# Column mean on one core: the wait of VectorE's second addition, the leader of the first section, and ScalarE waiting for the last pair's second rows

## The chip, the core and the metric

The kernel runs on one core of a Trainium2 chip. The core's engines each run their own queue of instructions and meet through semaphores: TensorE (PE in the profile; PEld its weight loads), VectorE (DVE), ScalarE (ACT), GpSimd (POOL) and SyncE (SP), which here issues nearly all DMA transfers. An entry such as DVEq is the engine's sequencer: waits, branches, raising of semaphores, drains. The metric is the device time of the program in microseconds (us), as the median of several runs; less is better.

## The reference

```python
def reference(x):            # x: 8192 x 8192, float32
    return np.mean(x, axis=0)
```

## The kernel before

`x` is read once, 268.4 MB. The 8192 rows are 64 slabs of 128 rows. Slabs 0 to 61 are read as 31 pairs: pair k is 256 rows, two to a partition, so that a partition gets 2 x 8192 numbers, the first rows and the second rows, in one tile of 128 x 16384 (`pair0`, `pair1`, `pair2` in turn, three buffers of 8.4 MB). The last two slabs, `slab` and `last`, go into the buffer of pair 28.

SyncE issues the loads (line 85). Pairs 0 to 27 come in one transfer each (pair 0 in two), pairs 28 to 30 in two, first and second rows, the second on semaphores `second[b]`. From pair 3 on each load waits for the semaphore `read` (line 80).

VectorE makes two additions of 128 x 8192 for a pair (helper `add`, line 54). `first_rows(b)` (63) adds the sum so far, which lies in the first half of the buffer before, to the pair's first rows; `second_rows(b)` (67) adds the pair's second rows to that. A running sum thus moves from buffer to buffer. The semaphore `summed` is 1 after a second addition and 0 after a first one, and orders the additions: the first waits for 1 (line 64), the second for 0 (line 68). That wait for 0 is an instruction of its own and also raises `read`: the buffer before may be loaded anew. Pairs 1 to 27 are a loop of 9 turns of three pairs (88 to 92), in which `take` (57) waits for the landing and takes it off the semaphore; pairs 28 and 29 follow unrolled (93 to 97).

The instructions up to there stand in a critical section (line 76), which is opened and closed by one engine for all engines in it: SyncE. At its end the others drain and tell the leader, which lets the work behind the section go on. A second section (line 100), led by VectorE, holds pair 30's first addition and the wait for its second rows.

What follows is in the order of the text, with waits put in by the framework. `behind` (112) puts an instruction behind the second section. SyncE loads `slab` in four pieces (158) and `last` in ten (161, sizes `PIECES`); the later pieces are each issued when an earlier one has landed. VectorE adds pair 30's second rows in four quarters (166), and `slab`'s last quarter to the fourth (168). TensorE sums over partitions by matmuls with a tile of ones (line 130): three wide groups of columns, each 4 x 512, from `before` (pair 30's buffer), `slab` and `last`; a fourth of 4 x 256; four narrow ones of 256 (`fold_wide`, `fold_narrow`, `close`). ScalarE and VectorE scale the sums (145, 147). GpSimd stores the three wide groups (`rw`, 192), SyncE the rest (`r3`, 196; `row`, 208).

Of the kernel before, what the change touches and what calls it, by code (L numbers as in the profile page):

```python
# [22 lines left out]
def kernel(  # L23
# [5 lines left out]
    nc = tc.nc  # L29
    P = nc.NUM_PARTITIONS  # L30
    R, C = x.shape
    n_slabs = R // P
    n_pairs = n_slabs // 2 - 1
# [11 lines left out]
    pairs = [pair_pool.tile([P, 2 * C], F32, name=f"pair{b}", tag=f"pair{b}") for b in range(3)]  # L45


    landed = [tc.alloc_semaphore(f"landed{b}") for b in range(3)]
    second = [tc.alloc_semaphore(f"second{b}") for b in range(BY_ROW)]
    summed = tc.alloc_semaphore("summed")  # L50
    read = tc.alloc_semaphore("read")

    def add(dst, a, b):
        return nc.vector.tensor_tensor(out=dst, in0=a, in1=b, op=ADD)  # L54

    def take(sem, n):
        nc.vector.wait_ge(sem, n).then_inc(sem, -n)  # L57

    def rows(k):
        src = x[2 * P * k : 2 * P * (k + 1), :]  # L60
        return src.rearrange("(p j) c -> p (j c)", j=2)

    def first_rows(b):
        nc.vector.wait_ge(summed, 1)
        add(pairs[b][:, 0:C], pairs[b][:, 0:C], pairs[b - 1][:, 0:C]).then_inc(summed, -1)

    def second_rows(b):
        nc.vector.wait_op(summed, 0, "sem-eq").then_inc(read, 1)
        add(pairs[b][:, 0:C], pairs[b][:, 0:C], pairs[b][:, C : 2 * C]).then_inc(summed, 1)

    n_loop = n_pairs - BY_ROW - 1
    assert n_loop % 3 == 0
    with tc.tile_critical(no_gpsimd_drain=True, sync_engine=mybir.EngineType.SP):
        for k in range(n_pairs):
            b = k % 3
            if k >= 3:
                nc.sync.wait_ge(read, k - 2)  # L80
            cut = FIRST if k == 0 else C if k >= n_pairs - BY_ROW else 2 * C
            for lo, hi in ((0, cut), (cut, 2 * C)):
                if lo < hi:
                    sem = second[b] if lo == C else landed[b]
                    nc.sync.dma_start(out=pairs[b][:, lo:hi], in_=rows(k)[:, lo:hi]).then_inc(sem, 16)
        take(landed[0], 32)
        add(pairs[0][:, 0:C], pairs[0][:, 0:C], pairs[0][:, C : 2 * C]).then_inc(summed, 1)
        with nc.vector.Fori(0, n_loop // 3):
            for b in (1, 2, 0):
                take(landed[b], 16)  # L90
                first_rows(b)
                second_rows(b)
        for k in range(n_loop + 1, n_pairs - 1):
            nc.vector.wait_ge(landed[k % 3], 16)
            first_rows(k % 3)
            nc.vector.wait_ge(second[k % 3], 16)
            second_rows(k % 3)
    last_b = (n_pairs - 1) % 3
    before = pairs[last_b]
    with tc.tile_critical(no_gpsimd_drain=True, sync_engine=mybir.EngineType.DVE) as section:  # L100
        nc.vector.wait_ge(landed[last_b], 16)
        first_rows(last_b)
        nc.vector.wait_ge(second[last_b], 16)
        nc.vector.wait_op(summed, 0, "sem-eq")


    ctx.enter_context(tc.manual_schedule())


    order = mybir.DependencyInfo(mybir.DependencyClass.NoSync, mybir.DependencyReason.DATA)  # L110

    def behind(ins):
        tc.add_manual_dep(ins.ins, section.name, order, reason="not ahead of the section")

    ones = const_pool.tile([P, 32], F32)
    behind(nc.gpsimd.memset(ones, 1.0))  # L116

    wide, lo = [], 0
# [35 lines left out]
    slab, last = tail[:, 0:C], tail[:, C : 2 * C]  # L154
    parts = [(lo, lo + w) for lo, w, _ in wide[:3]] + [(wide[3][0], C)]
    for lo in range(0, C, C // 4):
        hi = lo + C // 4
        behind(nc.sync.dma_start(out=slab[:, lo:hi], in_=x[r : r + P, lo:hi]))
    lo = 0
# [2 lines left out]
        lo += w  # L162


    for lo, hi in parts:
        add(before[:, lo:hi], before[:, lo:hi], before[:, C + lo : C + hi])
    lo, hi = parts[3]
    add(before[:, lo:hi], before[:, lo:hi], slab[:, lo:hi])

# [69 lines left out]
```

## Time and profile before

| what | value |
|---|---|
| median of 3 runs | 629.08 us (628.46 to 629.09) |
| the profiled execution | 629.22 us, span 627.2 us |
| DVE busy | 533.5 us (85%) |
| PE busy | 13.0 us (2%) |
| HBM read | 268.44 MB, mean 428 GB/s |
| additions of 128x8192 | 60, each 8.69 us |
| loads of pairs (line 85), issue to landing | median 29.7 us |
| TensorE's first matmul | 610.88 us |
| SyncE's issue of the last store | 624.47 us |

The span runs from the first to the last instruction that was profiled; times inside it count from its start. Lines give the kernel's source line, the engine, the operation, the tiles, and in brackets the idle time before and what ended it. "Landing" is the last of a transfer's semaphore updates.

### The profile page before, as it was taken

The numbers are of one execution on the slowest core, as the hardware profiler recorded it, in microseconds if no ns is written. First come the engines' busy times: TensorE is split into PE (matmuls) and PEld (weight loads), VectorE is DVE, ScalarE is ACT, GpSimd is POOL, SyncE is SP. The second block draws the span as 40 slices with busy tenths as digits, with TensorE's granted clock in tenths as the row PEclk, the third lists the DMA queues.
The fourth block names the chain that finished last, engine by engine and source line by source line (L and its number), as shares of the span: only waits on it lengthen the run. The fifth ranks groups of instructions, "written<-read, shape, count | busy, mean of one in ns | idle before, by whom it ended". The sixth has DMA issues, their size and how long they took to land. (4 is left out here: it accounts for less than half of the span.)

```text
span 627.2 us, 518 instructions
## 1 busy us (share of the span) xinstructions
PE 13.0 (2%) x108; PEld 4.6 (1%) x108; DVE 533.5 (85%) x67; ACT 4.1 (1%) x7; POOL 1.0 (0%) x6
## 2 busy tenths in 40 slices
PE   0000000000000000000000000000000000000007
PEld 0000000000000000000000000000000000000002
DVE  0538988889888899888898888988889888899995
ACT  0000000000000000000000000000000000000001
POOL 0000000000000000000000000000000000000000
PEclk9999999999999999999999999999999999999999
DMA  9999999999999999999999999999999999999997
GB/s 392 410 468 401 468 401 431 439 401 468 401 468 401 468 401 468 401 468 401 468 401 468 401 468 401 468 401 468 401 468 401 468 401 468 401 435 433 435 409 299
DMA packets 7115, 268.49 MB, mean 428 GB/s; under 512 B 957, under 2 KB 1473, under 8 KB 1866
## 3 DMA queue, kind: packets, MB, share of 16 engines
q1 hardware_dynamic: 7066, 268.45, 99.2%
q0 software_dynamic: 48, 0.02, 0.0%
q8 instruction: 1, 0.02, 0.0%
HBM read 268.44 MB, written 0.03 MB: 428 GB/s over the span
## 5 line engine op out<-in xcount | busy, mean ns | idle before, releaser
L54 DVE TENSOR_TENSOR pair<-pair,pair 128x8192 f32<-128x8192 f32 (+1 forms) x31 | 263.1, 8485 | 59.3 <-DVEq L57 58.3
L54 DVE TENSOR_TENSOR pair<-pair 128x8192 f32<-128x8192 f32 (+1 forms) x34 | 269.6, 7938 | 27.7 <-DVEq L57 22.8
L130 PE MATMUL wide<-pair,ones 128*32 128x512 f32 (+1 forms) x88 | 12.2, 661 | 610.9 <-DVE pair L54 610.9
L130 PEld LDWEIGHTS wide<-pair,ones 128*32 128x32 f32 x88 | 3.6, 126 | 617.9 <-issue 617.2
L145 ACT ACTIVATE rw<-wide 128x512 f32<-128x512 f32 x3 | 1.8, 598 | 619.5 <-PE wide L130 619.5
L147 DVE TENSOR_SCALAR row<-narrow 1x256 f32<-1x256 f32 x2 | 0.8, 416 | 3.9 <-PE narrow L130 3.8
L130 PE MATMUL narrow<-pair,ones 128*32 128x256 f32 (+3 forms) x20 | 3.3, 386 | 0.0
L192 POOL DMA_DIRECT2D out_dram<-rw x1 | 0.7, 697 | 622.7 <-ACT r L145 622.7
L130 PEld LDWEIGHTS narrow<-pair,ones 128*32 128x32 f32 x20 | 1.3, 109 | 1.1 <-issue 0.6
L145 ACT ACT_TABLE_LOAD x1 | 1.3, 1283 | 0.7 <-PEq L223 0.7
L145 ACT ACTIVATE row<-narrow 1x256 f32<-1x256 f32 x2 | 0.8, 376 | 0.0
L145 ACT ACTIVATE r<-wide 128x256 f32<-128x256 f32 x1 | 0.4, 378 | 0.0
L116 POOL MEMSET ones<- 128x32 f32 x1 | 0.1, 125 | 0.3 <-POOLq L223 0.3
L223 POOL MEMSET const-float32-0.0<- 128x1 f32 x1 | 0.1, 98 | 0.2 <-issue 0.2
L223 POOL MEMSET const-float32-1.0<- 128x1 f32 x1 | 0.1, 98 | 0.0
L223 POOL MEMSET const-bfloat16-1.0<- 128x1 bf16 x1 | 0.1, 98 | 0.0
L223 POOL MEMSET const-uint8-127<- 128x1 uint8 x1 | 0.1, 98 | 0.0
## 6 DMA issues: line engine op xcount, KB each, us to landing
pair<-in_x_dram SPq DMA_DIRECT2D x6, 4096.0 KB, 25.5
pair<-in_x_dram SPq DMA_DIRECT2D x7, 1024.0 KB, 11.3
pair<-in_x_dram SPq DMA_DIRECT2D x1, 7168.0 KB, 21.2
pair<-in_x_dram SPq DMA_DIRECT2D x3, 512.0 KB, 16.0
pair<-in_x_dram SPq DMA_DIRECT2D x27, 29.7
pair<-in_x_dram SPq DMA_DIRECT2D x3, 128.0 KB, 11.8
pair<-in_x_dram SPq DMA_DIRECT2D x1, 80.0 KB, 7.4
pair<-in_x_dram SPq DMA_DIRECT2D x1, 48.0 KB, 5.2
```

Of the source, the lines that this page charges most:

```text
L54: return nc.vector.tensor_tensor(out=dst, in0=a, in1=b, op=ADD)
L116: behind(nc.gpsimd.memset(ones, 1.0))
L130: nc.tensor.matmul(out=dst, lhsT=ones, rhs=src, skip_group_check=True, **flags)
L145: nc.scalar.mul(out=dst, in_=src, mul=inv_r)
L147: nc.vector.tensor_scalar(out=dst, in0=src, scalar1=inv_r, scalar2=None, op0=mybir.AluOpType.mult)
L192: nc.gpsimd.dma_start(out=out[0:W3].rearrange("(n g w) -> g n w", g=GROUPS, w=512), in_=rw.rearrange("(g r) (n w) -> g r n w", r=32, w=512 ...
L223: nc = _bacc.Bacc("TRN2", target_bir_lowering=False, num_devices=1)
```

## The change

- `first_rows`: the wait for `summed` is put on the addition. (In the built program it still stands as a separate instruction in front, together with the wait for the landing where that is unrolled.)
- `second_rows`: the wait for `summed` to be 0 is put on the addition itself; `read` is raised by an instruction of its own behind the addition.
- The first section is opened and closed by TensorE. VectorE's wait for pair 30's first rows now stands at its end.
- The second section holds only ScalarE's wait for pair 30's second rows, and ScalarE leads it.
- Pair 30's first addition stands outside the sections, in the framework's order. The four quarters wait for the second section through a semaphore of ScalarE's; other instructions that are kept behind the section are so by order alone. With the section on ScalarE, its table load for the scaling follows that wait in its queue.

```diff
     def first_rows(b):
-        nc.vector.wait_ge(summed, 1)
-        add(pairs[b][:, 0:C], pairs[b][:, 0:C], pairs[b - 1][:, 0:C]).then_inc(summed, -1)
+        ins = add(pairs[b][:, 0:C], pairs[b][:, 0:C], pairs[b - 1][:, 0:C])
+        ins.wait_op(summed, 1, "sem-ge").then_inc(summed, -1)
 
     def second_rows(b):
-        nc.vector.wait_op(summed, 0, "sem-eq").then_inc(read, 1)
-        add(pairs[b][:, 0:C], pairs[b][:, 0:C], pairs[b][:, C : 2 * C]).then_inc(summed, 1)
+        ins = add(pairs[b][:, 0:C], pairs[b][:, 0:C], pairs[b][:, C : 2 * C])
+        ins.wait_op(summed, 0, "sem-eq").then_inc(summed, 1)
+        nc.vector.sem_inc(read, 1)
...
-    with tc.tile_critical(no_gpsimd_drain=True, sync_engine=mybir.EngineType.SP):
+    with tc.tile_critical(no_gpsimd_drain=True, sync_engine=mybir.EngineType.PE):
...
-    last_b = (n_pairs - 1) % 3
+        last_b = (n_pairs - 1) % 3
+        nc.vector.wait_ge(landed[last_b], 16)
     before = pairs[last_b]
-    with tc.tile_critical(no_gpsimd_drain=True, sync_engine=mybir.EngineType.DVE) as section:
-        nc.vector.wait_ge(landed[last_b], 16)
-        first_rows(last_b)
-        nc.vector.wait_ge(second[last_b], 16)
-        nc.vector.wait_op(summed, 0, "sem-eq")
+    with tc.tile_critical(no_gpsimd_drain=True, sync_engine=mybir.EngineType.Activation) as section:
+        nc.scalar.wait_ge(second[last_b], 16)
...
-    order = mybir.DependencyInfo(mybir.DependencyClass.NoSync, mybir.DependencyReason.DATA)
-
-    def behind(ins):
-        tc.add_manual_dep(ins.ins, section.name, order, reason="not ahead of the section")
+    def behind(ins, wait=False):
+        kind = mybir.DependencyClass.Sync if wait else mybir.DependencyClass.NoSync
+        info = mybir.DependencyInfo(kind, mybir.DependencyReason.DATA)
+        tc.add_manual_dep(ins.ins, section.name, info, reason="the last pair's second rows")
...
+    behind(add(before[:, 0:C], before[:, 0:C], pairs[last_b - 1][:, 0:C]))
     for lo, hi in parts:
-        add(before[:, lo:hi], before[:, lo:hi], before[:, C + lo : C + hi])
+        behind(add(before[:, lo:hi], before[:, lo:hi], before[:, C + lo : C + hi]), wait=True)
```

## The prediction

> **What bounds the kernel now.** I read the page first (slices and DMA), then the table of stretches, SyncE's waits, VectorE's timeline from pair 27 on, and the moments of landing. The page:
>
> ```profile
> DMA  9999999999999999999999999999999999999997
> ...
> HBM read 268.44 MB, written 0.03 MB: 428 GB/s over the span
> ```
>
> The DMA engines are busy in every slice but the last. The stretches say it stage by stage (columns: stretch, length, busy us of PE, PEld, DVE, ACT, POOL, clock, DMA share, GB/s):
>
> ```profile
> 160.00:545.00 385.00, 0.00 (x0) 0.00 (x0) 346.91 (x40) 0.00 (x0) 0.00 (x0) 1.00 1.00 434
> 563.00:598.60 35.60, 0.00 (x0) 0.00 (x0) 34.90 (x5) 0.00 (x0) 0.00 (x0) 1.00 1.00 431
> 610.90:623.40 12.50, 12.50 (x105) 4.31 (x106) 8.78 (x4) 1.88 (x4) 0.00 (x0) 1.00 0.97 393
> 623.40:627.20 3.80, 0.48 (x6) 0.22 (x2) 0.83 (x2) 0.94 (x3) 0.70 (x1) 1.00 0.04 9
> ```
>
> The stream runs at 431 to 434 GB/s up to the last piece: a pair of 8.39 MB takes 19.3 us. VectorE needs 2 x 8.69 plus gaps, 17.6 us a pair, so it waits in the loop. In the last stretch TensorE is busy throughout while the stream still runs: three engines end nearly together there.
>
> ```profile
> SPq L85 <- DVEq L68: 558.8, 28, 48.0
> SPq L76 <- DVEq L76: 25.4, 1, 25.4
> ...
> SPq L234 <- DMA out_dram<-rw: 1.1, 1, 1.1
> ```
>
> SyncE's 558.8 us behind line 68 (the raising of `read`) look bad and aren't: the page gives a median of 29.7 us from a load's issue to its landing, and the transfer takes 19.3, so a load is queued about 10 us before its turn. The second line is the section's end, the third, for the store of `rw`, is one of the kernel's last.
>
> ```profile
> 545.60 8.69 DVE L54 TENSOR_TENSOR pair<-pair,pair 128x8192 f32<-128x8192 f32 x1 [1.77 <-DVEq L57]
> 554.44 8.69 DVE L54 TENSOR_TENSOR pair<-pair 128x8192 f32<-128x8192 f32 x1
> 563.27 8.69 DVE L54 TENSOR_TENSOR pair<-pair,pair 128x8192 f32<-128x8192 f32 x1
> 572.14 8.69 DVE L54 TENSOR_TENSOR pair<-pair 128x8192 f32<-128x8192 f32 x1 [0.17 <-DVE pair L54]
> 580.97 8.69 DVE L54 TENSOR_TENSOR pair<-pair,pair 128x8192 f32<-128x8192 f32 x1
> 589.84 8.69 DVE L54 TENSOR_TENSOR pair<-pair 128x8192 f32<-128x8192 f32 x1 [0.18 <-DVE pair L54]
> 599.18 8.69 DVE L54 TENSOR_TENSOR pair<-pair,pair 128x8192 f32<-128x8192 f32 x1 [0.66 <-DVEq L100]
> 608.49 8.89 DVE L54 TENSOR_TENSOR pair<-pair 128x2048 f32<-128x2048 f32 x4 [0.62 <-DVEq L100]
> 617.42 2.29 DVE L54 TENSOR_TENSOR pair<-pair,pair 128x2048 f32<-128x2048 f32 x1
> ```
>
> From 545.60 on VectorE never waits for data: its gaps are 0.14 to 0.18 us inside pairs and 0.66 and 0.62 at the sections. These gaps are what the change can shorten.
>
> **Part by part.** *First addition.* In the built program its wait on `summed` still stands as an instruction ahead of it: 0.
>
> *Second addition.* Its separate wait goes. Gaps of this kind are 0.15 (554.44 after 545.60 + 8.69), 0.17 and 0.18. What an addition with its own wait takes is shown at 617.42: the quarters before end at 608.49 + 8.89 = 617.38, so 0.04. Gain 0.11, 0.13, 0.14. In the loop this only lengthens the wait for the landing (1.74 to 1.84 us); pairs 27, 28 and 29 count: 0.38 us.
>
> *`read` raised behind the addition.* SyncE hears of the free buffer later by the start of the addition and one instruction, 0.02 to 0.1 us: line 88's first instruction, queued likewise behind an addition, starts 0.03 us after it. The 10 us of queue hide it; without that cover it would cost 28 times as much, 0.6 to 3 us.
>
> Whether VectorE's queue halts at the addition's wait shows at the end:
>
> ```profile
> L234 DVEq DRAIN  x1: 802/802/802, 623.6 to 623.6; - x1
> ```
>
> This drain, queued behind two scalings that wait for TensorE from 619.7 on, begins at 623.6, when the second one's matmul is done: the queue halted. The Trainium skill (Perfetto Trace Analysis, the section on DVE / Act engine instructions) says the opposite: the instruction goes into a wait queue and the sequencer is free for the next before the semaphores are met. By that rule `read` would rise as the pair lands, 8.8 us early; the trace disagrees, and the sum would be the same, since the stream is never empty.
>
> *TensorE leads the first section.* At the start SyncE waits for TensorE's first instruction rather than its own. SyncE's is at 0.73, its branch at 0.82, the first load at 0.97; VectorE hears of SyncE's at 0.79, so a hop is 0.06. TensorE leaves the opening barrier within 0.02 of SyncE, its instruction taking 0.05 against 0.02. Ends: -0.02 and +0.2; I take +0.05, near the hop. It shifts the whole stream. At the section's end the message goes VectorE, TensorE, VectorE rather than VectorE, SyncE, VectorE, and a NOP, a wait and a branch on VectorE fall away: 0.66 becomes 0.26 to 0.45, I take 0.31; gain 0.35.
>
> *Pair 30's first wait moved into the section.* SyncE's 14 loads (4 of `slab`, 10 of `last`) and TensorE queue behind it. The rows land at 572.1 + 21.7 = 593.8, the section ends with pair 29's second addition at about 598.1: 4.3 us of cover. The loads' issue, 598.7 now, gets a hop more and comes 0.4 earlier. Pair 30's second rows land at 572.4 + 31.0 = 603.4, and until then the stream has work: 4.7 us of cover, less the 1.0 us from the first issue (0.97) to the first packet (2.02).
>
> *Pair 30's second rows awaited by ScalarE.* They land at 603.4, with some 0.5 us for the section's end; VectorE asks at 607.1: hidden by about 3 us. The table load (1.28 us at 0.75 now) follows the section, at about 604, and is asked for at 619: hidden. On VectorE the wait, branch, drain and NOP of the old section (0.62) become one wait for pair 30's first addition, like line 68's 0.15: gain 0.47.
>
> *Sum.* VectorE's quarters start 0.38 + 0.35 + 0.47 = 1.20 us earlier, about 607.3, and TensorE at about 609.7 (now 610.88). Then what is late is the data. The first two pieces of `last` land at 600.5 + 15.3 = 615.8 and 600.9 + 17.3 = 618.2. TensorE would be at the second piece's matmuls at 617.85 (now 619.05) and waits for it, keeping 0.8 us. The last piece:
>
> ```profile
> L161 SPq DMA_DIRECT2D pair<-in_x_dram x1: 328/328/328, 618.2 to 618.2; - x1
> ...
> DMA to landing us min/median/max: 5.2/5.2/5.2
> ```
>
> It lands at 618.2 + 5.2 = 623.4 in either kernel, plus the start's 0.05, and its matmul runs at 623.55 now. Behind it stand the scaling, the store of `row` (issued at 624.47, landing at 626.1) and SyncE's last waits. `rw` is stored some 0.8 us sooner, but its landing (626.0) is only 0.1 before `row`'s. `row`'s own chain gains about 0.1 by VectorE's and ScalarE's earlier scalings having passed, and 0.05 by SyncE coming early to its last check: -0.15. Net 0.05 - 0.15 = -0.10. The profiled execution took 629.22 us (span 627.2 and 2.0 around it): 629.12. Its excess over the median, 0.14, is scatter: 629.08 - 0.10 = 629.0.
>
> TensorE's first groups of four matmuls start every 0.85 us until 615.1 and every 0.43 after it. If that slow phase ends at a fixed moment and not 4.2 us after the start, TensorE wins 0.6 instead of 1.2, and the end is the same. The Trainium skill (TensorE: Matmul & The Clock Gate, Part 1) has a free-running window of 3.4 us, by which the phase may last differently from run to run.
>
> **The rivals.** (a) *Slower: `read` counts only when the second addition has finished.* No row shows a raising that is queued behind an unfinished addition; for it speaks only the order in the code, against it line 88's instruction at 0.03 us and the section's drain, 8.70 us long, which would not be needed. After a landing: first addition 0.18 to 8.87, second to 17.6, issue at 17.7, first packet 1.05 later at 18.75; the packets ahead end at 19.3 less the 0.36 from last packet (623.02) to landing: 18.95. So it decides from an issue-to-packet time of 1.25 us. At 0 to 0.3 us of hole, 28 loads cost 0 to 8; at 0.2, 634.7 us. Chance 0.08.
>
> (b) *Slower: TensorE reaches its first instruction late.* 1.3 us or more, shifting the stream: 630.4 and up. Against it: the barrier before it already waits for TensorE (0.32 of 0.66 us). Chance 0.03.
>
> (c) *Faster: the end follows TensorE and not the landings.* The whole 1.20 and the 0.15 of the store's chain: 629.08 - 1.35 = 627.7. For it: TensorE has no gap until 622; against: the last matmuls start within 0.2 us of their landings. Chance 0.07.
>
> (d) *The queue runs ahead* at the new wait, as weighed above: SyncE's issues move 8.8 us forward, 629.0. Chance 0.05.
>
> **How the numbers follow.** Forecast (0.77) and (d) give no change: 629.0, from 628.3 (0.8 of TensorE's gain kept to the end) to 629.5 (start +0.2 and the scatter of 0.3). The range goes on to what I may have mis-sized at either end and to the lowest end of (a), 628.0 to 630.1; some 0.17 stays outside. A measurement of this kernel can tell about 0.2%, 1.26 us, from no change. Same 0.82, faster 0.07 (c), slower 0.11 ((a) and (b)).
>
> **What would show it.** Right: second additions 0.04 us behind the first; pair 30's first addition near 598.45, the quarters near 607.3, TensorE from 609.7 with gaps ahead of the pieces; SyncE's loads in the loop still about 29.7 us from issue to landing; last piece landing at 623.4. Wrong: loads 21 us from issue to landing and a DMA share under 1.00 in the loop (a); 38 us (d); a first load after 1.3 us (b); the last landing earlier than 623.

## The result and the profile after

The kernel after the change takes 628.01 us (median of 22 runs, 627.51 to 628.41), the kernel before 629.08 (22 runs, 628.01 to 629.47). The ratio is 0.9985, interval 0.9979 to 0.9992: 0.5 to 1.3 us faster, most likely 0.9. The same comparison on another chip gave 0.9988 (0.9979 to 0.9997). That lies within the 0.2% called no change, as forecast, but it is some ten times the 0.1 us that the sum gave, and 628.01 is only 0.01 us inside the low end of the range (628.0 to 630.1). The profiled execution of after took 627.87 us with a span of 626.1, against 629.22 and 627.2.

First the table of stretches of after (columns as in the prediction):

```profile
160.00:545.00 385.00, 0.00 (x0) 0.00 (x0) 346.26 (x40) 0.00 (x0) 0.00 (x0) 1.00 1.00 434
562.60:597.70 35.10, 0.00 (x0) 0.00 (x0) 34.77 (x4) 0.00 (x0) 0.00 (x0) 1.00 1.00 433
609.10:622.90 13.80, 13.56 (x105) 4.64 (x106) 9.04 (x5) 2.24 (x5) 0.66 (x1) 1.00 0.98 399
622.90:626.10 3.20, 0.53 (x6) 0.26 (x4) 0.56 (x2) 0.69 (x2) 0.03 (x1) 1.00 0.04 10
```

The stream runs as before, 433 to 434 GB/s at a DMA share of 1.00. From TensorE's start to the last landing it is now 13.8 us where it was 12.5, and TensorE works 13.56 of them: it has gaps. From the last landing to the end of the span it is 3.2 us where it was 3.8 (exactly: 3.14 and 3.79). GpSimd's 0.7 us, the issue of `rw`'s store, has gone from the last stretch into the one before.

VectorE's timeline from pair 27 on (start, length, in brackets the idle time before):

```profile
545.15 8.69 DVE L54 TENSOR_TENSOR pair<-pair,pair 128x8192 f32<-128x8192 f32 x1 [1.89 <-DVEq L57]
553.88 8.69 DVE L54 TENSOR_TENSOR pair<-pair 128x8192 f32<-128x8192 f32 x1
562.70 8.69 DVE L54 TENSOR_TENSOR pair<-pair,pair 128x8192 f32<-128x8192 f32 x1
571.43 8.69 DVE L54 TENSOR_TENSOR pair<-pair 128x8192 f32<-128x8192 f32 x1
580.26 8.69 DVE L54 TENSOR_TENSOR pair<-pair,pair 128x8192 f32<-128x8192 f32 x1
588.98 8.69 DVE L54 TENSOR_TENSOR pair<-pair 128x8192 f32<-128x8192 f32 x1
597.88 8.69 DVE L54 TENSOR_TENSOR pair<-pair,pair 128x8192 f32<-128x8192 f32 x1 [0.20 <-PEq L77]
606.67 8.89 DVE L54 TENSOR_TENSOR pair<-pair 128x2048 f32<-128x2048 f32 x4
615.60 2.29 DVE L54 TENSOR_TENSOR pair<-pair,pair 128x2048 f32<-128x2048 f32 x1
```

The second additions follow the first by 0.035 us (571.43 after 562.70 + 8.69 is 0.04), the sections' gaps of 0.66 and 0.62 are 0.20 and 0.10. From pair 27's first addition to the first quarter it is 61.53 us (606.67 - 545.15, with the trace's third decimal) instead of 62.89: 1.36 us gained. The last piece of `last`, though, has not come closer:

```profile
L160 SPq DMA_DIRECT2D pair<-in_x_dram x1: 328/328/328, 617.8 to 617.8; - x1
...
DMA to landing us min/median/max: 5.2/5.2/5.2
```

It is issued 0.4 us earlier than before (617.8, was 618.2) only because the whole stream was: pair 27's first addition starts at 545.15 and not 545.60. From that addition to the last landing it is 77.80 us, before 77.78. So the span's 1.08 us divide into 0.43 in the stream ahead of pair 27 and 0.65 behind the last landing. The rest of the profiled executions' difference, 0.27, is time around the span.

The chain of work that ended last shows who binds now:

```profile
597.87 7.61 DMA pair<-in_x_dram
605.49 0.02 issue
605.50 15.99 DMA pair<-in_x_dram
621.49 0.04 issue
621.54 0.64 PE wide L129 x8
622.17 1.27 PE narrow L129 x9
```

The landings lead until 621.49. In before the same chain ran through TensorE without a break from its first matmul:

```profile
610.88 8.34 PE wide L130 x56
...
623.06 0.49 PE narrow L130 x5
```

Last the stores, in the timeline of before and then of after. The first number is the issue:

```profile
623.61 0.70 POOL L192 DMA_DIRECT2D out_dram<-rw  x1 [622.75 <-ACT r L145]
623.62 0.78 ACT L145 ACTIVATE row<-narrow 1x256 f32<-1x256 f32 x2
623.62 0.67 SPq L196 DMA_DIRECT2D out_dram<-r  x1
624.47 0.29 SPq L208 DMA_DIRECT2D out_dram<-row  x1
```

```profile
622.24 0.70 POOL L192 DMA_DIRECT2D out_dram<-rw  x1 [621.37 <-ACT rw L144]
...
622.65 0.63 SPq L196 DMA_DIRECT2D out_dram<-r  x1
...
623.87 0.28 SPq L208 DMA_DIRECT2D out_dram<-row  x1
```

In before all three stores come within 0.86 us of each other and after the last landing (623.38). In after `rw`'s and `r3`'s are issued 0.71 and 0.30 us ahead of the last landing (622.95), and `row`'s has 1.63 us between it and `rw`'s. `row`'s store takes 1.63 us from issue to its last update in before (624.47 to 626.10) and 1.25 in after (623.87 to 625.12). SyncE's waits at the end agree:

```profile
SPq L234 <- DMA out_dram<-row: 0.4, 1, 0.4
...
SPq L234 <- DMA out_dram<-rw: 0.2, 1, 0.2
```

The wait for `rw`'s store was 1.1 us.

### The profile page after: what moved, and what is told of

It reads as the page before. It is cut to its first block, busy times and chain, and to the rows that moved or that the text cites. A ratio compares the mean times of both kernels' runs of the same rounds, so it can differ in the third digit from the quotient of the medians.

```text
span 626.1 us, 521 instructions
## 1 busy us (share of the span) xinstructions
PE 14.1 (2%) x108; PEld 5.0 (1%) x108; DVE 533.5 (85%) x67; ACT 4.2 (1%) x7; POOL 1.0 (0%) x6
## 6 DMA issues: line engine op xcount, KB each, us to landing
pair<-in_x_dram SPq DMA_DIRECT2D x27, 29.7
```

## The experiments

Two theories for the 0.65 us behind the last landing and the 0.43 ahead of it. **Theory A:** in before TensorE's wide groups are late, so that `rw` and `r3` are scaled and stored together with `row`; `row`'s store runs beside theirs and takes longer. Whatever brings the wide groups forward by enough makes the end shorter. **Theory B:** the loop's change (the second addition's own wait, `read` raised behind it) or the new leader makes the stream itself faster, and the end only follows. The kernels were timed in groups, each group beside runs of the kernel before on its own chip. The times are medians, "end" is from the last landing to the end of the span, "row" is from the issue of `row`'s store to its last update, "apart" from the issue of `rw`'s store to that of `row`'s (from printed times, good to 0.01 us), the last three in the profiled execution.

| kernel | us | against before | ratio (interval) | end | row | apart |
|---|---|---|---|---|---|---|
| before | 629.08 | | | 3.79 | 1.63 | 0.86 |
| before, second profile | 628.99 (one run) | | | 3.82 | 1.60 | 0.85 |
| after | 628.01 | -1.07 | 0.9985 (0.9979, 0.9992) | 3.14 | 1.25 | 1.63 |
| after, again | 628.03 | -0.77 | 0.9988 (0.9979, 0.9997) | 3.14 | 1.25 | 1.41 |
| before, new second addition | 628.76 | +0.21 | 1.0001 (0.9992, 1.0010) | 3.76 | 1.62 | 0.85 |
| after, old second addition | 628.25 | -0.30 | 0.9993 (0.9984, 1.0002) | 3.36 | 1.33 | 1.15 |
| after, VectorE 1.3 us later | 628.71 | +0.16 | 0.9998 (0.9990, 1.0007) | 3.96 | 1.62 | 0.86 |
| after, VectorE 0.6 us later | 628.03 | -0.52 | 0.9991 (0.9982, 1.0000) | 3.14 | 1.25 | 1.33 |
| before, TensorE warmed | 628.17 | -0.38 | 0.9993 (0.9984, 1.0002) | 3.17 | 1.26 | 1.23 |
| before, no store of `rw` | 628.27 | -0.53 | 0.9995 (0.9986, 1.0004) | 3.23 | 1.24 | none |
| after, SyncE leads | 628.13 | -0.67 | 0.9990 (0.9981, 0.9999) | 3.05 | 1.25 | 1.53 |

The kernel before spreads over 627.6 to 629.8 us in the groups, in two clusters (near 628.4 and 629.4), and the medians of its groups are 628.55, 628.80 and 628.55. A difference of 0.2 us between two rows is thus nothing. By its time alone, no row from the new second addition to the one without `rw`'s store can be told from before: the intervals all reach 1.0000. What follows therefore rests on the ends, one profiled execution of each kernel (two of before and of after). The forecasts in us were also made against 629.08, and the before of each group ran 0.3 to 0.5 us under that, so that a time can lie in its range for that reason alone.

**One part at a time.** Before with the new `second_rows` alone:

```diff
     def second_rows(b):
-        nc.vector.wait_op(summed, 0, "sem-eq").then_inc(read, 1)
-        add(pairs[b][:, 0:C], pairs[b][:, 0:C], pairs[b][:, C : 2 * C]).then_inc(summed, 1)
+        ins = add(pairs[b][:, 0:C], pairs[b][:, 0:C], pairs[b][:, C : 2 * C])
+        ins.wait_op(summed, 0, "sem-eq").then_inc(summed, 1)
+        nc.vector.sem_inc(read, 1)
```

> Before, with the second addition changed alone (its wait in itself, read raised behind it); sections as before. Theory A (the gain of 1.07 us is made behind the loop: VectorE's chain from pair 27 on is shorter, so TensorE's wide groups and the stores of rw and r3 come sooner): VectorE's quarters start 0.38 us earlier against the last landing, 628.7 to 628.9. Theory B (the loop's changed raising of read makes the stream itself end earlier, 622.95 instead of 623.38 in the two profiles): the whole of the stream's share and more, 628.1 to 628.5.

VectorE's chain from pair 27 to the first quarter went from 62.89 to 62.48 us, the 0.4 of the forecast, and the time did not move: 1.0001. (628.76 is in theory A's range only because before ran at 628.55 beside it.) The 0.4 us bring the stores' issue only to 0.20 us after the last landing (before: 0.24). The reason is in the timeline of TensorE's weight loads, which has a row for each of its first groups of matmuls; these are the sixth and seventh row of before, then the seventh and eighth of this kernel:

```profile
615.12 0.18 PEld L130 LDWEIGHTS wide<-pair,ones 128*32 128x32 f32 x4 [0.63 <-issue]
615.60 0.14 PEld L130 LDWEIGHTS wide<-pair,ones 128*32 128x32 f32 x4 [0.29 <-issue]
```

```profile
614.58 0.14 PEld L131 LDWEIGHTS wide<-pair,ones 128*32 128x32 f32 x4 [0.62 <-issue]
615.01 0.14 PEld L131 LDWEIGHTS wide<-pair,ones 128*32 128x32 f32 x4 [0.29 <-issue]
```

TensorE starts 0.41 us earlier (64.87 us after pair 27's first addition, in before 65.28), but takes six slow steps of 0.85 us instead of five, so its seventh row comes 69.96 us after that addition, in before 70.00: the slow phase ate the gain.

The changed kernel with the old `second_rows` (the same diff the other way round):

> The changed kernel with the second addition as before (separate wait that raises read): sections and leaders changed alone. Theory A: the gaps at pair 30 (0.66 to 0.20 and 0.62 to 0.10 in the two profiles) bring 0.97 of the 1.36 us, 628.2 to 628.4. Theory B: nothing in the loop differs from before, 629.0 to 629.2.

The chain is 61.93 us, 0.96 less than before, `rw`'s store is issued 0.32 us ahead of the last landing, and the end is 3.36. The sections thus bring most of the end's gain and the two parts together all of it, but the parts don't add up in proportion: 0.41 us of chain gave nothing, 0.96 gave 0.43 of the end, 1.36 gave 0.65. TensorE takes six slow steps in this kernel too.

**Giving VectorE's gain back.** The changed kernel with an addition of 1.3 us in VectorE's queue ahead of the quarters (its result is overwritten later):

```diff
     behind(add(before[:, 0:C], before[:, 0:C], pairs[last_b - 1][:, 0:C]))
+    add(rw[:, 0:1180], before[:, 0:1180], before[:, 0:1180])
```

> The changed kernel with one more VectorE addition of 128x1180 (1.30 us, result not used) between pair 30's first addition and the quarters: VectorE's gain behind the loop is given back, nothing else. Theory A: the gain goes, 628.9 to 629.2. Theory B: the stream is as in the changed kernel, 628.0 to 628.2.

The chain is back at 62.94 us, and with it everything at the end:

```profile
623.26 0.69 POOL L193 DMA_DIRECT2D out_dram<-rw  x1 [622.40 <-ACT r L144]
623.27 0.63 SPq L197 DMA_DIRECT2D out_dram<-r  x1
...
624.12 0.28 SPq L209 DMA_DIRECT2D out_dram<-row  x1
```

`row`'s store is again 0.86 us behind `rw`'s and takes 1.62 us. The loop of this kernel is the changed one, and its time is before's (0.9998): theory B falls as the cause of the end.

The same with 0.59 us (500 columns instead of 1180):

> The changed kernel with one more VectorE addition of 128x500 (0.59 us, result not used) ahead of the quarters: half of the delay of the run with 1.30 us. If the gain behind the last landing comes by row's store getting clear of the others (theory A): rw and r3 are issued about 0.3 us ahead of the last landing as in the run with the sections alone, row's store takes 1.25 to 1.35 us, the end 3.15 to 3.4 us behind the last landing, 628.1 to 628.4. If the gain goes in proportion to VectorE's lead: 3.45 us and 628.4 to 628.6.

```profile
622.51 0.69 POOL L193 DMA_DIRECT2D out_dram<-rw  x1 [621.65 <-ACT rw L144]
...
622.63 0.63 SPq L197 DMA_DIRECT2D out_dram<-r  x1
...
623.84 0.28 SPq L209 DMA_DIRECT2D out_dram<-row  x1
```

Just over half of VectorE's gain (0.71 of 1.36 us) is given back and the end stays at 3.14 us: 1.33 us between `rw`'s store and `row`'s do as much as the 1.63 of after.

**TensorE alone.** The kernel before with five matmuls ahead of the wide groups, on data of `slab` that is long there, so that TensorE's slow steps (0.85 us each) are over, from 605.8 to 610.1 us, before the wide groups begin:

```diff
+    for n in range(5):
+        mm(narrow[0][3][0:32, :], slab[:, 0:512], start=True, stop=True)
     for n in range(3):
         fold_wide(n, before, start=True, stop=False)
```

> Before with 5 more matmuls of 512 columns on slab's first piece (landed at 606) ahead of the wide groups, results not used: TensorE's slow phase of 4.2 us begins at 606 instead of 610.9, VectorE as before. Theory A in the form that TensorE is late (its groups start every 0.85 us at first): the groups end up to 2 us sooner, stores as early as in the changed kernel, 628.0 to 628.3. Theory A in the form that VectorE's earlier quarters matter by themselves: 628.9 to 629.1. Theory B: 629.0 to 629.2.

VectorE's chain is before's (62.89 us) and nothing of the loop or the sections is changed, yet the end is 3.17 us and `row`'s store takes 1.26:

```profile
622.84 0.70 POOL L194 DMA_DIRECT2D out_dram<-rw  x1 [621.97 <-ACT r L145]
622.85 0.67 SPq L198 DMA_DIRECT2D out_dram<-r  x1
...
624.07 0.29 SPq L210 DMA_DIRECT2D out_dram<-row  x1
```

So the late wide groups are the place, as theory A says, and VectorE is only one way to bring them forward.

**Which store is in the way.** The kernel before without GpSimd's store of `rw`:

```diff
-    nc.gpsimd.dma_start(
-        out=out[0:W3].rearrange("(n g w) -> g n w", g=GROUPS, w=512),
-        in_=rw.rearrange("(g r) (n w) -> g r n w", r=32, w=512)[:, 0],
-    )
```

> Before with GpSimd's store of rw left out, so that three quarters of the output are not written; all else as before. It measures row's store by itself: if the store of rw under way lengthens it, it takes 1.25 us from issue to landing instead of 1.63 and the time falls by 0.3 to 0.5 us; if it takes 1.63 whatever else is under way, the end moves by less than 0.15 us.

```profile
623.25 0.67 SPq L192 DMA_DIRECT2D out_dram<-r  x1
624.10 0.29 SPq L204 DMA_DIRECT2D out_dram<-row  x1
```

`r3`'s and `row`'s stores stand as they do in before, 0.85 us apart and late, but `row`'s takes 1.24 us and the end is 3.23. It is `rw`'s store that lengthens `row`'s by 0.38 us, and `r3`'s doesn't.

**The leader.** The changed kernel with SyncE leading the first section, as in before (`EngineType.PE` back to `EngineType.SP`):

> The changed kernel with SyncE as the first section's leader, as before. The first load is issued at 0.97 instead of 1.03, the stream shifts by 0.06; the section's end costs VectorE some 0.1 us more or less. Both too small for the time: within 0.2 us of the changed kernel. If TensorE's lead were what brought the gain: back to before's time.

The first load is issued at 0.97 us again (1.03 with TensorE), and the time is 628.13 against 628.03 beside it: TensorE's lead costs its 0.06 us at the start and gives nothing that can be measured.

**The changed kernel again**, in the group of the last two:

> The changed kernel once more, beside before on the chip of this group, for the size of the gain. Theory A (tail alone): from the last piece's landing to the end 3.1 us against 3.8 of before (3.14 and 3.79 in the first two profiles), 0.5 to 0.7 us faster by the median. Theory B (stream too): 1.0 to 1.1 us, with pair 27 reached before 545.2 and the stretch from there to the last landing under 77.6 us.

The end is again 3.14 us, with `row`'s store at 1.25. Pair 27's first addition starts at 545.36 us and the last landing comes 77.79 us after it, so neither sign of theory B is there; the median gained 0.77 us.

**The changed kernel with TensorE warmed**, four matmuls of 512 columns placed as above:

> The changed kernel with 4 more matmuls of 512 columns on slab's first piece ahead of the wide groups, results not used: TensorE's slow phase begins at 605.5 instead of 609.1. If TensorE was still late in the changed kernel: 0.2 to 0.5 us faster than it. If the landings bind there (theory A): within 0.15 us of it, 3.0 to 3.15 us from the last landing to the end.

It took 629.28 us, 1.25 more than the changed kernel beside it; neither theory had that. The end is 3.16 us, as it should be. What is late is the last landing: 79.04 us after pair 27's first addition, where all kernels so far have 77.77 to 77.94. The records of the last piece show why: 15 of its 16 updates come by 623.08, the sixteenth at 624.34. One of the 16 DMA engines is late, by 1.26 us, behind a fetch of instructions, a single packet of 16 KB that takes 0.93 us, from 621.83 to 622.76. The records of packets don't name the engine, but their order points to it: no other data packet starts after 622.73, and the late engine's share of the last three pieces then runs as one file from 622.741, 16 ns before the fetch ends, to 623.90, each packet starting a few ns before the end of the one ahead of it. The next kernel's packets do the same (fetch to 622.741, file from 622.727).

**A longer TensorE program without the warming**, four matmuls of 32 columns instead:

```diff
+    for n in range(4):
+        mm(narrow[0][3][0:32, 0:32], slab[:, 0:32], start=True, stop=True)
```

> The changed kernel with 4 more matmuls of only 32 columns on slab's first piece, results not used: as many instructions in TensorE's queue as in the run with 4 of 512 columns, which was 1.2 us slower, but no warming and hardly any reading. If an instruction fetch of 16 KB (0.93 us on one DMA engine, at 621.83 there, at 622.42 in the changed kernel) moves ahead of the last pieces because TensorE's program is longer: fetch near 621.9, the last three pieces 1.2 to 1.4 us late, 629.0 to 629.5. If the long matmuls' reading or power disturbed the stream: 627.9 to 628.2.

629.22 us, last landing again 79.05 us after pair 27's first addition, the fetch at 621.81. The last two pieces in the DMA issues from 600 us on, in this kernel and then in after (the last column is us from issue to landing):

```profile
pair<-in_x_dram SPq DMA_DIRECT2D x1, 80.0 KB, 8.7
pair<-in_x_dram SPq DMA_DIRECT2D x1, 48.0 KB, 6.4
```

```profile
pair<-in_x_dram SPq DMA_DIRECT2D x1, 80.0 KB, 7.4
pair<-in_x_dram SPq DMA_DIRECT2D x1, 48.0 KB, 5.2
```

From issue to landing both pieces take 1.2 to 1.3 us more. The fetch is in the profiles of before and after and of the other kernels of the table too, equally long, but there it begins only 0.53 to 0.60 us ahead of the last landing and ends after it: the pieces don't wait for it.

**What sets the fetch's moment**: the changed kernel with SyncE leading and the four matmuls of 512, which takes the section's four instructions out of TensorE's queue again:

> The changed kernel with SyncE as the first section's leader and the 4 matmuls of 512 columns: TensorE's queue is about as long as in the changed kernel alone. If the fetch is what cost 1.2 us: it comes after the last pieces' data again, 627.7 to 628.1, with TensorE ready well ahead of each piece (3.0 us from the last landing to the end). If the long matmuls cost it: 629.0 to 629.5.

629.48 us, the fetch at 621.54, last landing 79.02 us after pair 27's first addition: the fetch did not go back, as the forecast by TensorE's length had it. The length of TensorE's program doesn't decide it, then: its trace has 239 TensorE records of matmuls, weight loads and others here and 243 in the two kernels ahead, but 244 in before with five matmuls more, whose fetch is late and harmless (622.67). No run moved the fetch by itself; that it is the cause rests on the order of the packets and on an early fetch and the 1.2 us going together in three kernels of three and in none of the others. What sets its moment stays open.

**The kernel before once more**, to see whether its two clusters of times differ at the end:

> The kernel before, a second profiled execution. The times of its runs lie in two groups, near 628.4 and near 629.4 us. If only the stream scatters (theory A with a moving stream), the stretch from the last landing to the end of the span is 3.7 to 3.8 us whatever the time, the store of row takes 1.6 us, and a lower time comes with an earlier last landing. If the end scatters too, an execution near 628.4 us shows that stretch at 3.1 to 3.4 us, and the changed kernel gains by always having the short end.

The execution took 628.99 us, between the clusters, with an end of 3.82 us and `row`'s store at 1.60. So the end is the same in two profiles of before; no execution near 628.4 was seen in a profile, and what parts the clusters stays open.

## Why the prediction was right and wrong

**Right, by its steps.** The second additions: 0.035 us where 0.04 was taken. The section's end 0.20 (0.31), the second section 0.10 (0.15), the start 0.06 (0.05), VectorE's quarters 1.36 us earlier (1.20). `read` behind the addition cost nothing: loads still take a median of 29.7 us from issue to landing. The last landing stands where it stood beside the stream (77.80 us after pair 27's first addition, before 77.78), and the change in time stays inside 0.2%. In the span the last landing came at 622.95, earlier than the 623 that the prediction named as a sign of being wrong; pair 27 was reached 0.46 us earlier in that execution, which the changed kernel does not do in general (below).

**Luck.** That 628.01 is in the range at all is luck: the low end was 628.3 if 0.8 us of TensorE's gain is kept to the end, and 0.3 us further for what might be mis-sized; 0.02 us more and the time would have been outside. The measured time is nearer to rival (c)'s 627.7 than to the forecast's 629.0.

**The rivals.** (a) is refuted: `read` is raised with the second addition's start, not its end. The trace has the raising of pair 27 at 553.888, 13 ns after the addition's start, and the 21 us from issue to landing of (a) didn't come. All 29 raisings of the kernel come 13 to 15 ns after their addition's start. (d) is refuted by the same line, as 8.7 us ahead of it would be needed: an instruction queued behind an addition that waits does not pass it. The Trainium skill (Perfetto Trace Analysis, DVE / Act Engine Instruction) has the sequencer ready for the next instruction while one stands in the wait queue; if it was, the raising still did not run ahead here. (b): the first load went out 0.06 us later, far from 1.3. (c) gave 627.7 by an end that follows TensorE; the last landing still leads, so it didn't come in full, but a part of it did: in before the chain that ended last ran through TensorE, and the stores of its earlier groups followed it.

**The step that failed** is the end: "`row`'s own chain gains about 0.1 by VectorE's and ScalarE's earlier scalings having passed, and 0.05 by SyncE coming early to its last check: -0.15." The mechanism was in view and one term was mis-sized: `row`'s store was held at the 1.63 us that it took in before. It measured:

| term | forecast | measured |
|---|---|---|
| `row`'s store issued nearer to the last landing | -0.1 | -0.17 (1.09 to 0.92) |
| `row`'s store, issue to last update | 0 | -0.38 (1.63 to 1.25) |
| SyncE's last waits | -0.05 | -0.10 (the rest of 0.65) |

The 1.63 us were the price of a store beside another one, `rw`'s, issued 0.86 us before it. The sum moved that other store 0.8 us away, and said so, but only asked when it would land. The kernel before with warmed TensorE and the one without `rw`'s store show it from two sides.

Hence also the sentence on TensorE's slow phase, "the end is the same", was wrong: TensorE's late groups were what pushed the stores together, and taking the slow phase away did as much for the end of before (3.17) as the whole change (3.14). Not wrong was that it may last differently: the steps of 0.85 us last 4.24 us in some executions (before, 610.88 to 615.12) and 5.09 in others (before with the new second addition, 609.49 to 614.58; the changed kernel has had both). The granted clock in the rows is 1.00 throughout, but the trace's own clock records begin only where the spacing halves, at 615.21 us in before and 613.58 in after. The Trainium skill (TensorE: Matmul & The Clock Gate, Part 1) has a half clock until a busy window of some 3.4 us has passed, at a moment that the start doesn't set; the halved spacing (0.85 to 0.43) agrees with it, and so do 4.24 and 5.09 us, as an estimate from that window gives between one and two of them, 3.4 to 6.8 us.

**What stays open.** The end explains 0.65 us of a difference measured at 0.77 to 1.07. The rest, 0.1 to 0.4, is of the size of the scatter of the stream: pair 27's first addition starts at 544.62 to 545.60 us over the profiles, in no order by kernel (before with the new second addition has the earliest, before the latest). Before's runs scatter more than after's (standard deviations 0.41 to 0.55 against 0.21 to 0.27); before with warming and before with the new second addition scatter less too (0.25 each), and the two kernels with VectorE held back more (0.69 and 0.53). Why was not settled.

## What to carry to other kernels

When two ends are nearly level, put not only the issue of the last transfer into the sum but what runs beside it: a store's duration read from the trace is its duration beside its neighbours of that execution, and a change that moves the neighbours changes it. Gain on an engine that is not the bound can still pay by taking its stores out of the last one's way; here that was worth 0.4 us once they stood some 1.2 us apart, and no more beyond that. Look for single 16 KB instruction fetches in the last microseconds when an innocent added instruction costs more than it takes.

## What the runs showed of the hardware

- A store of 4 KB (`row`) takes 1.24 to 1.26 us from issue to its last update when the 24 KB store of `rw` was issued 1.23 us or more before it or not at all, 1.33 at 1.15 us, and 1.60 to 1.63 at 0.85 to 0.86 us.
- An instruction fetch of 16 KB, one packet, takes 0.93 us on one DMA engine; in the three kernels where it came ahead of the last pieces, one engine's last update came 1.24 to 1.27 us after those of the other fifteen, and the whole kernel waited.
- On VectorE a wait carried by the addition costs 0.035 us between two additions, a wait of its own 0.15 to 0.18.
- TensorE's matmuls go by steps of 0.85 us for 4.24 or 5.09 us from the first one, depending on the execution, and by 0.43 after it; an engine that feeds TensorE earlier can lose the gain to a longer slow phase, as 0.41 us became 0.04.
